# Batch norm and ReLU on one core: the second half of x as one load in the middle, the first half's remainder last

## The chip, the core and the metric

The kernel runs on one core of a Trainium2 chip. The metric is the device time of one execution in microseconds (us). Before the change the median of 8 runs was 83.8 us, from 83.51 to 83.95.

## The reference

`x` is a float32 tensor of shape 32 x 128 x 32 x 32 (16.78 MB). Each of the 128 channels has its own `gamma`, `beta`, `running_mean` and `running_var`:

```python
normalized = (x - running_mean[None, :, None, None]) / np.sqrt(running_var[None, :, None, None] + eps)
scaled = normalized * gamma[None, :, None, None] + beta[None, :, None, None]
return np.maximum(scaled, 0).astype(np.float32)
```

Every element is read once and written once, so 16.78 MB go in and 16.78 MB go out. For each element the work is one multiply, one add and one maximum.

## The kernel before

**Layout.** The tensor is seen as 4096 rows (batch times channel) of `HW` = 1024 floats, 4 KB each. They are split into `T` = 2 halves `t`; in each half, partition `p` of 128 holds `J` = 16 consecutive rows `j`. One partition's 16 rows of a half are 64 KB in one piece of memory. All of `x` fits on the chip at once, so every tile has its own buffer (`bufs=1`), and no load ever waits for a buffer to come free.

**Tiles and loads.** `TILES` lists pieces `(t, a, b)`: rows `a` to `b` of half `t`, in the order in which they are loaded and computed. The sync engine (SP) issues all loads at the start (L56), one DMA per tile, except where `LOAD_CUTS` splits a tile. Before the change there are six loads: of 2, 2, 4 and 8 rows from the first half, and two of 8 rows from the second. In a DMA each partition's rows are one contiguous run, so the six loads consist of runs of 8, 8, 16, 32, 32 and 32 KB, 128 of each.

**Parameters.** The scalar engine (ACT) issues four small DMAs (L63). TensorE spreads the parameters over the partitions (L78), ACT and VectorE (DVE) turn them into a scale and a bias (L86 to L94).

**Compute and stores.** ACT then passes over the rows in the order of `TILES`. One activation, L102, does a row in place (`HALVES` names rows that are done in two halves). After the last row of a tile, or ahead of a row named in `STORE_CUTS`, ACT itself issues the store of the rows since the last store (L110). This order is written out by hand (`manual_schedule`): ACT's queue holds the passes and the store issues in program order. The six stores before the change have runs of 4, 4, 8, 16, 32 and 64 KB per partition; the last is the whole second half.

**Queues.** Loads go through SP's DMA queue (q1 in the profile), stores and parameters through ACT's (q10). Both feed the same 16 DMA engines; each engine serves 8 of the 128 partitions, so a load or a store gives each engine 8 runs. A DMA's completion is counted on one of eight semaphores, used in turn, and a new DMA on a used semaphore waits for that semaphore's previous DMA.

Of the kernel before, what the change touches and what calls it, by code (L numbers as in the profile page):

```python
# [1 line left out]

# [4 lines left out]


F32 = mybir.dt.float32
ACTF = mybir.ActivationFunctionType  # L10

J = 16

TILES = ((0, 0, 2), (0, 2, 4), (0, 4, 8), (0, 8, 16), (1, 0, 16))

LOAD_CUTS = {(1, 8)}
STORE_CUTS = {(0, 1)}

HALVES = {(0, 0), (0, 1)}


@with_exitstack
def kernel(
    ctx: ExitStack,
    tc: tile.TileContext,
    x: bass.AP,
    gamma: bass.AP,
    beta: bass.AP,  # L30
    running_mean: bass.AP,
    running_var: bass.AP,
    eps: bass.AP,
    out: bass.AP,
):
    nc = tc.nc
    B, C, H, W = x.shape
    HW = H * W
    P = nc.NUM_PARTITIONS
    assert C % J == 0 and P % (C // J) == 0 and (B * C) % (P * J) == 0  # L40
    Q = C // J
    T = B * C // (P * J)

    xr = x.rearrange("b c h w -> (b c) (h w)").rearrange("(t p j) w -> t p j w", p=P, j=J)
    outr = out.rearrange("b c h w -> (b c) (h w)").rearrange("(t p j) w -> t p j w", p=P, j=J)

    data = ctx.enter_context(tc.tile_pool(name="data", bufs=1))
    params = ctx.enter_context(tc.tile_pool(name="params", bufs=1))
    psum = ctx.enter_context(tc.tile_pool(name="psum", bufs=1, space=bass.MemoryType.PSUM))

    tiles = []
    for t, a, b in TILES:
        xt = data.tile([P, b - a, HW], F32, name=f"x{t}_{a}")
        cuts = [a] + [j for j in range(a + 1, b) if (t, j) in LOAD_CUTS] + [b]
        for c, d in zip(cuts, cuts[1:]):
            nc.sync.dma_start(out=xt[:, c - a : d - a, :], in_=xr[t, :, c:d, :])  # L56
        tiles.append((t, a, b, xt))

    raw = params.tile([Q, 4, J], F32, name="raw")
    for k, src in enumerate((running_var, gamma, running_mean, beta)):
        nc.scalar.dma_start(out=raw[:, k, :], in_=src.rearrange("(q j) -> q j", j=J))  # L63
    eps_t = params.tile([P, 1], F32, name="eps_t")
    nc.vector.memset(eps_t, float(eps))  # L65
    rep = params.tile([Q, P // Q, Q], F32, name="rep")
    nc.gpsimd.memset(rep, 1.0)  # L67
    nc.gpsimd.affine_select(  # L68
        out=rep,
        in_=rep,  # L70
        compare_op=mybir.AluOpType.is_equal,
        fill=0.0,
        base=0,
        pattern=[[0, P // Q], [-1, Q]],
        channel_multiplier=1,
    )
    cols = psum.tile([P, 4, J], F32, name="cols")
    nc.tensor.matmul(  # L78
        cols.rearrange("p k j -> p (k j)"),
        rep.rearrange("q r s -> q (r s)"),  # L80
        raw.rearrange("q k j -> q (k j)"),
        start=True,
        stop=True,
    )
    std_t = params.tile([P, J], F32, name="std_t")
    nc.scalar.activation(out=std_t, in_=cols[:, 0, :], func=ACTF.Sqrt, bias=eps_t[:, 0:1], scale=1.0)  # L86
    rstd_t = params.tile([P, J], F32, name="rstd_t")
    nc.vector.reciprocal(out=rstd_t, in_=std_t)  # L88
    scale_t = params.tile([P, J], F32, name="scale_t")
    nc.vector.tensor_mul(out=scale_t, in0=cols[:, 1, :], in1=rstd_t)  # L90
    ms_t = params.tile([P, J], F32, name="ms_t")
    nc.vector.tensor_mul(out=ms_t, in0=cols[:, 2, :], in1=scale_t)  # L92
    bias_t = params.tile([P, J], F32, name="bias_t")
    nc.vector.tensor_sub(out=bias_t, in0=cols[:, 3, :], in1=ms_t)  # L94

    with tc.manual_schedule(engines={mybir.EngineType.Activation}):
        for t, a, b, xt in tiles:
            first = a
            for j in range(a, b):
                step = HW // 2 if (t, j) in HALVES else HW  # L100
                for w in range(0, HW, step):
                    nc.scalar.activation(  # L102
                        out=xt[:, j - a, w : w + step],
                        in_=xt[:, j - a, w : w + step],
                        func=ACTF.Relu,
                        bias=bias_t[:, j : j + 1],
                        scale=scale_t[:, j : j + 1],
                    )
                if j + 1 == b or (t, j + 1) in STORE_CUTS:
                    nc.scalar.dma_start(  # L110
                        out=outr[t, :, first : j + 1, :], in_=xt[:, first - a : j + 1 - a, :]
                    )
                    first = j + 1


# [1 line left out]
_INS = ['x', 'gamma', 'beta', 'running_mean', 'running_var', 'eps']  # L117
_OUTS = [((32, 128, 32, 32), 'float32')]

_NUMBERS = {'eps': 1e-05}  # L120


# [26 lines left out]
```

## Time and profile before

| what | value |
|---|---|
| median of 8 runs | 83.8 us (83.51 to 83.95) |
| profiled execution, its own time | 83.45 us |
| span of the profiled execution | 81.7 us |
| ACT busy | 39.1 us (48% of the span) |
| bytes read, written | 16.78 MB, 16.78 MB |
| mean rate over the span | 410 GB/s |
| q1 (loads), share of 16 engines | 48.6% |
| q10 (stores, parameters), share of 16 engines | 47.8% |
| first load issued, last store issued | 0.81 us, 55.98 us |

The span is what the profiler saw of the kernel's instructions; the profiled execution's own time is 1.7 us more. The two shares of the DMA queues add up: each engine serves one queue at a time. All other engines together are busy less than 3 us.

### The profile page before, as it was taken

The page shows a single profiled execution, that of the slowest core. Times are in us where ns is not written, and L with a number is a line of the kernel's source. Part 1 is how long each engine was busy: PE and PEld are TensorE (multiplying, and loading weights), DVE is VectorE, ACT ScalarE, POOL GpSimd, SP SyncE. Part 2 cuts the span into 40 slices and gives each one's busy share as a digit, 9 for nine tenths or more (in the row PEclk, how much of TensorE's full clock was granted, in tenths as well). Part 3 has the DMA queues.
Part 4 walks back from the last instruction along what each step waited for, and adds up shares of the span by engine and source line. Part 5 has one row for each costly group of instructions (what it writes and reads, how often), then busy time and mean ns, then how long its engine had stood idle before and what let it go on. Part 6 is the DMA issues. An engine that isn't in the chain of part 4 may idle for free.

```text
span 81.7 us, 120 instructions
## 1 busy us (share of the span) xinstructions
PE 0.7 (1%) x2; PEld 0.5 (1%) x2; DVE 0.8 (1%) x5; ACT 39.1 (48%) x36; POOL 0.8 (1%) x6
## 2 busy tenths in 40 slices
PE   0003000000000000000000000000000000000000
PEld 0002000000000000000000000000000000000000
DVE  0000300000000000000000000000000000000000
ACT  0600477799239999199995199993000000000000
POOL 3000000000000000000000000000000000000000
DMA  3899999989999999969789699997992999997490
GB/s 44 317 417 481 409 417 481 481 385 463 403 417 449 395 471 393 505 297 601 321 369 593 281 449 425 513 465 305 513 770 96 417 513 513 513 513 321 192 513 0
DMA packets 1792, 33.56 MB, mean 411 GB/s; under 512 B 256, under 2 KB 256, under 8 KB 512
## 3 DMA queue, kind: packets, MB, share of 16 engines
q1 hardware_dynamic: 864, 16.78, 48.6%
q10 hardware_dynamic: 928, 16.78, 47.8%
HBM read 16.78 MB, written 16.78 MB: 410 GB/s over the span
## 4 chain that ended last, share of the span: by engine, by line
DMA 56%; ACT 10%; issue 2%; SPq 0%
DMA x<-in_x_dram 56%; ACT x L102 10%; SPq L56 0%
## 5 line engine op out<-in xcount | busy, mean ns | idle before, releaser
L102 ACT ACTIVATE x<-x,bias_t,scale_t 128x1024 f32<-128x1024 f32 (+1 forms) x34 | 37.5, 1177 | 10.0 <-DMA x<-in_x_dram 7.6
L86 ACT ACT_TABLE_LOAD x1 | 1.3, 1283 | 2.6 <-issue 2.6
L86 ACT ACTIVATE std_t<-cols,eps_t 128x16 f32<-128x16 f32 x1 | 0.3, 274 | 4.3 <-PE cols L78 4.3
L78 PE MATMUL cols<-raw,rep 8*128 8x64 f32 x2 | 0.7, 428 | 7.5 <-DMA raw<-in_beta_dram 7.5
L78 PEld LDWEIGHTS cols<-raw,rep 8*128 8x128 f32 x2 | 0.5, 308 | 7.5 <-issue 7.5
L68 POOL TENSOR_SCALAR_AFFINE_SELECT rep<-rep 8x128 f32<-8x128 f32 x1 | 0.4, 392 | 0.1
L88 DVE RECIPROCAL rstd_t<-std_t 128x16 f32<-128x16 f32 x1 | 0.3, 252 | 7.6 <-ACT std_t L86 7.6
L67 POOL MEMSET rep<- 8x128 f32 x1 | 0.2, 194 | 0.3 <-POOLq L130 0.3
L90 DVE TENSOR_TENSOR scale_t<-cols,rstd_t 128x16 f32<-128x16 f32 x1 | 0.2, 175 | 0.1
L92 DVE TENSOR_TENSOR ms_t<-cols,scale_t 128x16 f32<-128x16 f32 x1 | 0.2, 175 | 0.0
L94 DVE TENSOR_TENSOR bias_t<-cols,ms_t 128x16 f32<-128x16 f32 x1 | 0.2, 175 | 0.0
L130 POOL MEMSET const-bfloat16-1.0<- 128x1 bf16 x1 | 0.1, 107 | 0.0
L130 POOL MEMSET const-uint8-127<- 128x1 uint8 x1 | 0.1, 107 | 0.0
L130 POOL MEMSET const-float32-0.0<- 128x1 f32 x1 | 0.1, 104 | 0.3 <-issue 0.3
L130 POOL MEMSET const-float32-1.0<- 128x1 f32 x1 | 0.1, 104 | 0.0
L65 DVE MEMSET eps_t<- 128x1 f32 x1 | 0.1, 59 | 0.9 <-PEq L130 0.9
## 6 DMA issues: line engine op xcount, KB each, us to landing
x<-in_x_dram SPq DMA_DIRECT2D x3, 4096.0 KB, 38.7
out_dram<-x ACTq DMA_DIRECT2D x1, 4096.0 KB, 28.6
x<-in_x_dram SPq DMA_DIRECT2D x2, 1024.0 KB, 5.8
x<-in_x_dram SPq DMA_DIRECT2D x1, 2048.0 KB, 11.2
out_dram<-x ACTq DMA_DIRECT2D x1, 2048.0 KB
out_dram<-x ACTq DMA_DIRECT2D x2, 512.0 KB, 18.6
out_dram<-x ACTq DMA_DIRECT2D x1, 1024.0 KB
raw<-in_running_var_dram ACTq DMA_DIRECT2D x1, 0.5 KB
```

Source lines behind the costliest of these rows:

```text
L65: nc.vector.memset(eps_t, float(eps))
L67: nc.gpsimd.memset(rep, 1.0)
L68: nc.gpsimd.affine_select(out=rep, in_=rep, compare_op=mybir.AluOpType.is_equal, fill=0.0, base=0, pattern=[[0, P // Q], [-1, Q]], channel ...
L78: nc.tensor.matmul(cols.rearrange("p k j -> p (k j)"), rep.rearrange("q r s -> q (r s)"), raw.rearrange("q k j -> q (k j)"), start=True, s ...
L86: nc.scalar.activation(out=std_t, in_=cols[:, 0, :], func=ACTF.Sqrt, bias=eps_t[:, 0:1], scale=1.0)
L88: nc.vector.reciprocal(out=rstd_t, in_=std_t)
L90: nc.vector.tensor_mul(out=scale_t, in0=cols[:, 1, :], in1=rstd_t)
L92: nc.vector.tensor_mul(out=ms_t, in0=cols[:, 2, :], in1=scale_t)
L94: nc.vector.tensor_sub(out=bias_t, in0=cols[:, 3, :], in1=ms_t)
L102: nc.scalar.activation(out=xt[:, j - a, w : w + step], in_=xt[:, j - a, w : w + step], func=ACTF.Relu, bias=bias_t[:, j : j + 1], scale=sc ...
L130: nc = _bacc.Bacc("TRN2", target_bir_lowering=False, num_devices=1)
```

## The change

`TILES` is put in another order and cut differently. After the two loads of 2 rows, the whole second half (16 rows, runs of 64 KB) is loaded by one DMA. Then rows 4 to 12 of the first half follow (runs of 32 KB), and rows 12 to 16 last (runs of 16 KB). ACT computes and stores in this order; the second half is stored in two DMAs of 8 rows. Row 1 of the first tile is done by one activation instead of two.

```diff
-TILES = ((0, 0, 2), (0, 2, 4), (0, 4, 8), (0, 8, 16), (1, 0, 16))
+TILES = ((0, 0, 2), (0, 2, 4), (1, 0, 16), (0, 4, 12), (0, 12, 16))
 
-LOAD_CUTS = {(1, 8)}
-STORE_CUTS = {(0, 1)}
+LOAD_CUTS = set()
+STORE_CUTS = {(0, 1), (1, 8)}
 
-HALVES = {(0, 0), (0, 1)}
+HALVES = {(0, 0)}
```

There are now five loads, with runs of 8, 8, 64, 32 and 16 KB, and seven stores, with runs of 4, 4, 8, 32, 32, 32 and 16 KB.

## The prediction

> **What bounds the kernel now.** I read the page first: the slices, the queues' shares and the chain.
>
> ```profile
> DMA  3899999989999999969789699997992999997490
> GB/s 44 317 417 481 409 417 481 481 385 463 403 417 449 395 471 393 505 297 601 321 369 593 281 449 425 513 465 305 513 770 96 417 513 513 513 513 321 192 513 0
> ...
> q1 hardware_dynamic: 864, 16.78, 48.6%
> q10 hardware_dynamic: 928, 16.78, 47.8%
> ...
> DMA 56%; ACT 10%; issue 2%; SPq 0%
> ```
>
> The two queues hold the 16 DMA engines for 48.6 + 47.8 = 96.4% of the span, 78.8 us of 81.7. The dips in the slices (6, 2, 4) are no idle time: a run of 64 KB takes longer than a slice of 2.04 us, and 96 GB/s stands right behind 770. The chain is followed through one load and ACT and doesn't show this; its 56% is not the share that DMA bounds. Next the stretches:
>
> ```profile
> 24.00:34.00 10.00, 0.00 (x0) 0.00 (x0) 0.00 (x0) 9.02 (x8) 0.00 (x0) 1.00 0.96 411
> 34.00:46.00 12.00, 0.00 (x0) 0.00 (x0) 0.00 (x0) 9.16 (x8) 0.00 (x0) 1.00 1.01 430
> 46.00:56.00 10.00, 0.00 (x0) 0.00 (x0) 0.00 (x0) 9.16 (x8) 0.00 (x0) 1.00 1.02 437
> 61.00:80.50 19.50, 0.00 (x0) 0.00 (x0) 0.00 (x0) 0.00 (x0) 0.00 (x0) 1.00 0.95 410
> ```
>
> The last two columns are DMA share and GB/s: about 1.0 with loads and stores mixed (24 to 46) and with stores alone. ACT, the fourth busy column, is nearly full up to 56 and then has nothing left, 25 us before the end. The timeline gives the order, and the waits say who waits:
>
> ```profile
> 0.81 7.54 SPq L56 DMA_DIRECT2D x<-in_x_dram  x6
> ...
> 11.05 0.37 ACTq L110 DMA_DIRECT2D out_dram<-x  x1
> ...
> 23.86 9.16 ACT L102 ACTIVATE x<-x,bias_t,scale_t 128x1024 f32<-128x1024 f32 x8 [3.01 <-DMA x<-in_x_dram]
> ...
> 46.80 9.16 ACT L102 ACTIVATE x<-x,bias_t,scale_t 128x1024 f32<-128x1024 f32 x8 [2.84 <-DMA x<-in_x_dram]
> 55.98 0.34 ACTq L110 DMA_DIRECT2D out_dram<-x  x1
> ```
>
> ```profile
> ACT x L102 <- DMA x<-in_x_dram: 7.6, 3, 3.0
> ...
> SPq L144 <- DMA out_dram<-x: 72.4, 4, 38.7
> ```
>
> ACT waits for loads, and the end waits for stores. Everything is issued long before it is moved: all loads by 8.4 us, though the last lands at 46; the last store at 56, though its first run starts at 61. So the bound is the total of the runs on a DMA engine.
>
> The trace's packet records (one for each contiguous run) give that total. A run takes 0.159 us for 4 KB, 0.309 for 8, 0.611 for 16, 1.213 for 32 and 2.418 for 64 KB, as load or store alike (64 KB was only stored). Doubling the size adds twice the bytes at 27.2 GB/s; what is over is some 0.008 us a run. The runs of one engine follow each other without a gap: the first starts at 1.82 us, the last ends at 80.57. That is 78.75 us, made up of 77.90 for its 96 runs at the durations above, 0.55 for the slow first runs before 4 us, 0.20 for 32 KB loads that took longer than 1.213, and 0.10 of gaps. With 1.82 us ahead and 1.18 behind, this is the span of 81.75; with the 1.7 us around it, 83.45, which is 0.35 below the median.
>
> **The change, part by part.** *The runs.* Before, each engine has 8 loads each of 8, 8, 16, 32, 32, 32 KB and 8 stores each of 4, 4, 8, 16, 32, 64: loads 16 x 0.309 + 8 x 0.611 + 24 x 1.213 = 38.94, stores 16 x 0.159 + 8 x (0.309 + 0.611 + 1.213 + 2.418) = 38.95. After, loads are 8 x (0.309 + 0.309 + 2.418 + 1.213 + 0.611) = 38.88, stores 16 x 0.159 + 8 x 0.309 + 24 x 1.213 + 8 x 0.611 = 39.02. Both sums are 77.90: it is the same set of sizes, with the 64 KB runs changed from store to load. Cost zero, if a 64 KB load runs like a 64 KB store.
>
> *64 KB loads.* No row shows one. From above: loads of 32 KB lost 0.20 us over 24 runs of an engine, 0.0083 each, while 8 and 16 KB after the start lost nothing, nor did any store. If the loss grew fourfold with each doubling, the new loads would lose 8 x 0.033 + 8 x 0.0083 = 0.33, 0.13 more than now. The slowest single 32 KB load ran at 23.8 GB/s; all 64 KB loads at that rate (2.76 us) would cost 8 x 0.34 = 2.7 us. From below: the loss goes with reading 32 KB runs, of which 8 remain of 24, which saves 0.13; with the gaps gone too, 0.2. I take zero, since the nearest row, the 64 KB store, runs at full rate (27.1 GB/s), and because the losses came in a few bursts (20.3, 40.0, 44.7 us) in which most engines lost something, not run by run.
>
> *Store issues and ACT.* What could cost is a dry store queue after the last load. Without the store of (1,0:8), an engine has all loads and the three small stores: the first 2 MB end at 7.5 us as now, the other loads take 8 x 4.242 = 33.9, the small stores 16 x 0.159 + 8 x 0.309 = 5.0, so work until 46.4 whatever the order. When does that next store come? The 64 KB loads take 19.3 us, to 26.9; store runs share from some 14.8 (issued at 11.05, the first store's runs began at 14.6 to 14.9), one per load run, five in all, so 27.7. ACT starts 0.7 later (now the last load run ends at 46.09, ACT resumes at 46.80) at 28.4, does 8 passes in 9.16, and issues at 37.6. With a lag of 3.6 (11.05 to 14.6) its first run could start at 41.2: 5.2 us to spare. Its 9.7 us of runs then cover from 46.4 to 56.1; the next store is issued at 47.2, ready at 50.8. The following needs 8 passes more: 56.8, ready 60.4, needed 65.8. The last: 4 passes, 61.8, ready 65.4, needed 75.5. Each has 5 us or more, so nothing on the path. If this cover were gone, each us of lateness would be a us at the end.
>
> How the engines share matters for that margin. In the records, 32 KB load runs alternate with single 4 KB store runs, at times two or three in a row: 16 stores among 17 loads from 13.6 to 35.5 us on one engine. The Trainium skill's page "DMA: Bandwidth & Descriptors", section "Queues, rings and completion order", says instead that an engine takes turns by packets, typically 9 to 17 descriptors. By that rule each small store would leave in one turn, all three during the 64 KB loads. Independently of the rule, the extreme is that all 5.0 us of small stores go ahead of the end of the second half: it ends at 26.9 + 5.0 = 31.9, its store is ready at 45.4 instead of 41.2, and 1.0 us of the margin is left. By row or rule the end stays.
>
> *ACT's passes.* Row 1 in one pass (1.15 us) and not two (1.52 with the gap) advances the second store's issue by 0.3 us; the queue is full of loads then. ACT's long pause up to 28.4 replaces the pauses of 3.0, 1.8 and 2.8. Hidden by the same loads: nothing.
>
> *Issues.* SP issues five loads (0.33 to 0.63 us each). The program's order shows the fourth and fifth waiting for parameter DMAs, which land by 7.5; the queue is filled up to 27 by then. Nothing waits behind them on SP. On ACT, store issues wait for semaphores of the parameters, of loads already computed, and the last for the first store's; all done many us before. The first two loads and the parameters keep their places, so the slow start stays. The last store again uses the semaphore that the last one used, so I leave the 1.18 us of the end alone.
>
> The sum: 0.00 for the runs, 0.00 for the rest, on the profiled 83.45; on the median, 83.8.
>
> **The rivals.**
>
> *Slower: 64 KB loads lose rate.* For: only loads lost anything, and only at the largest size loaded. Against: the 64 KB store has no loss. The place is the 8 runs of an engine between 7.5 and 28 us. From 0.021 us a run (8 x 0.021 = 0.17) it is measurable. At twice the average loss per us of today's 32 KB loads it is the +0.13 above; three times that extra, 0.4, gives 84.2; the far end is 86.5.
>
> *Slower: a dry queue.* For: nothing is stored between 28 and 38. Against: 5 us of margin. It needs ACT or the landing 5 us late; at 6 us late it gives 84.6.
>
> *Faster: the load losses go.* For: they sit in 32 KB loads, of which two thirds go. The full 0.2 and part of the gaps: 83.55. More can't be had, since all else is the runs themselves and the start and end.
>
> *The change isn't what it says:* the program's order shows it as told, so no chance is set aside.
>
> **How the numbers follow.** A measurement can tell about 0.2% (0.17 us) from no change. No change in the end: 0.49. Load losses gone, far enough to be seen: 0.20. 64 KB loads slower: 0.24; dry queue or another late store: 0.07. Faster is thus 0.20, same 0.49, slower 0.31. The forecast's own range is 83.65 to 83.95. For 8 in 10 it reaches down to the full saving and up to the 84.2 of the first rival; left out are its far end and the dry queue.
>
> **What would show it.** Right: runs without gaps from 1.8 to about 80.6, 64 KB loads at 2.42 us, queue shares adding up to 96%, last store issued near 62 with ACT idle behind it, one ACT wait of some 12 us ahead of 28. Wrong: 64 KB loads above 2.44, any engine idle near 46, or a first run later than 1.8.

## The result, and the profile after

The changed kernel takes 84.0 us (median of 22 runs, 83.83 to 84.15); the kernel before, over all its runs here, 83.64 us (62 runs, 83.35 to 84.06). The ratio is 1.004, interval 1.0029 to 1.005: slower by 0.36 us. The profiled execution of the changed kernel took 84.01 us with a span of 82.3.

The page after, with the rows shown of before: the slices, the queues and the chain.

```profile
DMA  2899991999919796969999989997997998998991
GB/s 48 334 427 721 510 446 64 541 541 541 476 66 541 319 542 287 573 287 470 334 414 398 550 350 414 510 478 334 462 494 334 446 510 350 414 510 366 422 406 80
...
q1 hardware_dynamic: 720, 16.78, 48.8%
q10 hardware_dynamic: 1072, 16.78, 47.5%
...
ACT 36%; DMA 32%; issue 3%; ACTq 1%; SPq 1%
```

The queues' shares still add up to 96.3%; the low slices early on (64 and 66 GB/s) follow high ones and are the 64 KB loads, booked by their start. The chain now walks through ACT, which is not the bound. The timeline and the two waits:

```profile
28.43 9.16 ACT L102 ACTIVATE x<-x,bias_t,scale_t 128x1024 f32<-128x1024 f32 x8 [13.04 <-DMA x<-in_x_dram]
37.61 0.34 ACTq L110 DMA_DIRECT2D out_dram<-x  x1
...
47.19 0.34 ACTq L110 DMA_DIRECT2D out_dram<-x  x1
...
56.76 0.34 ACTq L110 DMA_DIRECT2D out_dram<-x  x1
...
61.81 0.34 ACTq L110 DMA_DIRECT2D out_dram<-x  x1
```

```profile
ACT x L102 <- DMA x<-in_x_dram: 13.0, 1, 13.0
...
SPq L144 <- DMA out_dram<-x: 73.7, 4, 49.7
```

The end of ACT's pause and the four store issues are where the prediction's working put them, to 0.1 us. The difference is in the stretches (same columns as before: DMA share and GB/s last):

```profile
24.00:34.00 10.00, 0.00 (x0) 0.00 (x0) 0.00 (x0) 5.58 (x5) 0.00 (x0) 1.00 0.96 406
34.00:46.00 12.00, 0.00 (x0) 0.00 (x0) 0.00 (x0) 11.58 (x12) 0.00 (x0) 1.00 0.98 397
46.00:56.00 10.00, 0.00 (x0) 0.00 (x0) 0.00 (x0) 9.58 (x10) 0.00 (x0) 1.00 1.05 454
```

From 34 to 46 us the engines are as occupied as before (0.98), but move 397 GB/s where they moved 430. (Runs are booked where they start, so a few per cent of this are the edges of the stretch.) The packet records give the exact sum. *Nominal* is each run at its duration from the trace of before; *load loss* below is always what the loads after 4 us took beyond 0.309, 0.611, 1.213 and 2.418 us a run. "Per engine" is a sixteenth of the sum over all records. Two profiles of each kernel, the second ones from the experiments:

| us per engine | before | before again | after | after again |
|---|---|---|---|---|
| first run to last end | 78.75 | 78.92 | 79.33 | 79.24 |
| nominal sum of the 96 runs | 77.90 | 77.90 | 77.90 | 77.90 |
| slow runs before 4 us | 0.55 | 0.48 | 0.47 | 0.46 |
| load loss after 4 us | 0.20 | 0.43 | 0.77 | 0.70 |
| gaps, engines not ending together | 0.10 | 0.11 | 0.19 | 0.18 |

On average the time from first run to last end, below called the *transfer time*, grew by 0.45 us, of which 0.42 is load loss. What lies outside it did not change: the profiled execution's own time less the transfer time is 4.70 and 4.69 us before, 4.68 and 4.69 after. Stores lost nothing in any of the four. In the changed kernel the loss sits at few places: 0.16 and 0.19 at the eighth 64 KB run (25 us), and 0.57 and 0.44 in the 16 KB runs between 38.8 and 46.3 us. The 32 KB loads between lost 0.00 and 0.03.

### The profile page after: what moved, and what is told of

Read it like the earlier page. It is cut to its first block, busy times and chain, and to the rows that moved or that the text cites. A ratio compares the mean times of both kernels' runs of the same rounds, so it can differ in the third digit from the quotient of the medians.

```text
span 82.3 us, 119 instructions
## 1 busy us (share of the span) xinstructions
PE 0.7 (1%) x2; PEld 0.6 (1%) x2; DVE 0.8 (1%) x5; ACT 38.8 (47%) x35; POOL 0.8 (1%) x6
## 4 chain that ended last, share of the span: by engine, by line
ACT 36%; DMA 32%; issue 3%; ACTq 1%; SPq 1%
ACT x L102 36%; DMA x<-in_x_dram 32%; ACTq L110 1%; SPq L56 1%
```

## The experiments

The first theory to test was S (64 KB load runs lose rate), against M (short load runs lose where they meet short store runs) and T (stalls at moments of their own).

The variants differ in one more thing. By their profiles, the time outside the transfer time is 4.7 us in both kernels, e2 and e4, but 4.9 in e1, e3, e8, e12, f2, f3 and f4, 4.95 in e9, 5.0 in e7, 5.1 in e10 and f1 and 5.2 in e11. Up to 0.5 us of a variant's time, more than the effect of the change, is thus not in its runs; why is not known. What bears on the cause is the load loss, not the ratio.

**e1: the 64 KB load as two of 32 KB.**

```diff
-LOAD_CUTS = set()
+LOAD_CUTS = {(1, 8)}
```

> The changed kernel with the second half loaded by two DMAs with runs of 32 KB instead of one with 64 KB; all else as changed. Theory S (64 KB load runs lose rate): the loss between 7 and 28 us (0.19 us an engine in the changed kernel's packet records) goes to near 0, and the time falls by about 0.2 us, to 83.8. Theory M (16 KB load runs lose where they take turns with short store runs at the end of the loads, 0.57 us an engine): no change there, time stays at 84.0 (0.4% above before). Theory T (stalls of all engines at moments of their own, whatever the runs): same loss in total, 84.0.

Measured 84.28 us, ratio 1.0092 (1.0064 to 1.012): slower still; 0.2 us of the further 0.28 lies outside the transfer time. The load loss is 0.83, all of it in 32 KB runs, 0.00 in the 16 KB ones, though some of these ran between 8 KB stores. S failed, and M with it.

**e2: rising sizes at the end.**

```diff
-TILES = ((0, 0, 2), (0, 2, 4), (1, 0, 16), (0, 4, 12), (0, 12, 16))
+TILES = ((0, 0, 2), (0, 2, 4), (1, 0, 16), (0, 4, 8), (0, 8, 16))
```

> The changed kernel with the first half's remainder loaded as 4 rows and then 8 (runs of 16 KB, then 32 KB) instead of 8 and then 4. Theory M: the last load runs, which meet the 8 KB stores, are now 32 KB ones, the 16 KB ones meet 4 KB stores at 28 to 33 us; the 0.57 us falls to 0.2 or less and the time to 83.6 to 83.7. Theory S: 64 KB loads are still there, 84.0. Theory T: 84.0.

Measured 83.88 us, 1.0033 (1.002 to 1.0046). The loss, 0.63, moved on: 0.19 at the eighth 64 KB run again, 0.36 at the eighth and last 32 KB run. The falling sizes cost at most some 0.1 us.

**e3: the kernel before, second half as one 64 KB load.**

```diff
-LOAD_CUTS = {(1, 8)}
+LOAD_CUTS = set()
```

> The kernel before with the second half loaded by one DMA (64 KB runs) at the end; order and stores as before. Theory S: 8 runs of 64 KB lose some 0.2 us an engine beside the 0.1 that 32 KB loads lose now, time 0.1 to 0.2 us above before. Theory M: the loads keep long runs to the end, same as before within 0.1 us. Theory T: as before.

Measured 87.01 us, 1.0409 (1.0386 to 1.0432); no theory had it. Its timeline, and a stretch of it:

```profile
45.43 18.21 ACT L102 ACTIVATE x<-x,bias_t,scale_t 128x1024 f32<-128x1024 f32 x16 [12.47 <-DMA x<-in_x_dram]
63.66 0.34 ACTq L110 DMA_DIRECT2D out_dram<-x  x1
```

```profile
62.00:64.50 2.50, 0.00 (x0) 0.00 (x0) 0.00 (x0) 1.63 (x2) 0.00 (x0) 1.00 0.00 0
```

With nothing of the second half landed before 45 us, ACT needs 18.2 us until its one store, and the engines stand still from 62.2 to 64.5. This is the dry queue: some 2.4 us of the 3.4. Most of the rest is load loss, 1.05, of which 0.89 at the last 64 KB run; 0.2 lies outside the transfer time.

**e4: the small stores held back** to the first store of the second half (`HELD` names them).

```diff
+HELD = {(0, 1), (0, 2), (0, 4)}
...
+                    if (t, j + 1) not in HELD:
+                        for dst, src in held:
+                            nc.scalar.dma_start(out=dst, in_=src)
```

> The changed kernel with its three small stores (rows 0, 1 and 2 to 4) held back and issued with the first store of the second half, at some 37 us, so that loads run alone up to 39 us or so and hardly any load run meets a store run. Theories M and T in the form that loads lose only beside stores: the loss of loads after 4 us falls from 0.77 us to under 0.2 and the time to 83.4 to 83.5, below before. Theory S: the loss of the 64 KB runs, 0.19, stays, since it is due to their size; 83.6. If stalls come at moments of their own and hit loads alone as well: 84.0.

Measured 84.06 us, 1.0052 (1.0033 to 1.0072). The hold worked otherwise than meant:

```profile
27.84 1.24 ACT L105 ACTIVATE x<-x,bias_t,scale_t 128x1024 f32<-128x1024 f32 x1 [13.34 <-DMA x<-in_x_dram]
27.92 1.35 ACTq L117 DMA_DIRECT2D out_dram<-x  x3
```

The three stores stand behind eight passes in program order, but were issued when the first of these had just begun: they wait only for their own rows. Still it shows something: while loads ran alone, to 31.7 us, the 64 KB and 32 KB runs lost 0.00. From there to the end of the loads 0.36 were lost. The median stayed near the changed kernel's because first runs (0.64) and unequal ends (0.50 with the gaps) took what the loads saved.

**e5, e6: both kernels profiled again.**

> The changed kernel itself, profiled a second time. Theory T (stalls come at moments of their own): the long load runs stand elsewhere than at 24.9, 40.1 and 44.1 us, and their sum differs from 0.77 us an engine by some tenths. Theory P (stalls follow from which runs are read and written together): the same runs are long again (the eighth 64 KB load, the third and sixth or so of the 16 KB loads), with about the same sum.

> The kernel before itself, profiled a second time. Theory P: the loss of its loads after 4 us is again near 0.20 us an engine, in small pieces near 20, 40 and 44.5 us. Theory T: the pieces stand elsewhere and the sum is anything between 0.1 and 0.6 us (its times spread over 0.7 us, from 83.35 to 84.06).

The runs are the same, their losses vary (table above): after, 25 and 40 us again (0.19, and 0.30 for 0.25), 44 us with 0.05 for 0.22; before, 0.05 at 20 us both times, 0.22 for 0.03 at 40. The times were 83.93 and 83.61. T in the form of moments unrelated to the runs falls; the place follows the sequence, the amount only partly. Fixed moments counted from the start would repeat too; against them stand f2 and e10 below, in which loads and stores ran side by side to 51.9 and 54.5 us and lost 0.00 after 30 us.

**e7: small stores behind the first store of the second half**, which does wait for its passes (e4 with the held stores in another order).

```diff
+                        for dst, src in held[-1:] + held[:-1]:
```

> The changed kernel with its three small stores issued behind the first store of the second half, which itself waits for eight passes: nothing is stored before some 39 us, and loads run alone until then. If loads lose only beside stores: no loss from 8 to 39 us, in all at most 0.2 us an engine, and the time is 83.4 to 83.6, at or a little below before. If loads lose by themselves (by size, or at moments of their own): some 0.5 us or more is lost and the time stays at 84.0.

Measured 85.12 us, 1.0165 (1.014 to 1.0191). Loads alone from 8 to 37 us lost 0.00, as the first reading said; then 1.3 us were lost at once, not the 0.2 at most of that reading. Two stretches:

```profile
28.00:36.00 8.00, 0.00 (x0) 0.00 (x0) 0.00 (x0) 8.00 (x8) 0.00 (x0) 1.00 0.97 418
...
38.00:42.00 4.00, 0.00 (x0) 0.00 (x0) 0.00 (x0) 3.36 (x3) 0.00 (x0) 1.00 1.06 315
```

Engines fully occupied at 315 GB/s: that is a load loss seen on a view. Stores were issued from 36.7 us, but the first store run started at 41.1. The 16 KB load runs five to seven, the last ones ahead of an engine's first 32 KB store run, took about 1.0 us on average in place of 0.61. Of the 1.35 us, 0.84 were lost in load runs that had ended before any store run began: store runs beside them can't be what made these long.

**e8: the order alone**, with the load sizes of before.

```diff
-TILES = ((0, 0, 2), (0, 2, 4), (1, 0, 16), (0, 4, 12), (0, 12, 16))
+TILES = ((0, 0, 2), (0, 2, 4), (1, 0, 16), (0, 4, 8), (0, 8, 16))
-LOAD_CUTS = set()
+LOAD_CUTS = {(1, 8)}
```

> The order alone: the second half ahead of the first half's last 12 rows, but with the load sizes of the kernel before (32 KB twice for the second half, then 16 KB and 32 KB). If the place of the second half carries the loss: 0.5 us or more an engine in loads and 84.0 or above. If the sizes carry it (64 KB in the middle, 16 KB at the end): 0.2 us and 83.6 as before.

Measured 84.31 us, 1.0076 (1.0053 to 1.0099), load loss 0.71. With after, e1 and e2 this makes a square:

| ratio to before | last loads 32, 16 KB | last loads 16, 32 KB |
|---|---|---|
| second half as one 64 KB load | 1.004 (the change) | 1.0033 (e2) |
| second half as two 32 KB loads | 1.0092 (e1) | 1.0076 (e8) |

In load loss the same four are 0.77 and 0.70 (the change), 0.63 (e2), 0.83 (e1) and 0.71 (e8), against 0.20 and 0.43 before: the order carries the loss. The single 64 KB load takes back only some 0.1 us of it, less than the two profiles of before differ (0.23). The upper row is faster by 0.3 to 0.4 us in good part for another reason: by the profiles, e1 and e8 spend 0.2 us more outside the transfer time. Falling or rising makes no clear difference.

**e9: no overlap.** The kernel before, all stores held behind one of the second half's first six rows, in e7's order of issue.

```diff
+HELD = {(0, 1), (0, 2), (0, 4), (0, 8), (0, 16)}
-STORE_CUTS = {(0, 1)}
+STORE_CUTS = {(0, 1), (1, 6)}
```

> The kernel before (its loads and their order) with all stores held until six rows of the second half are done, at some 39.4 us; a store of those six rows goes first, the five others behind it, the remaining ten rows last. Loads run alone to their end at some 41. If all loss of loads comes from stores beside them: under 0.1 us an engine lost in loads, at most some 0.5 us of dry engines between loads and stores, and the time within 0.2 us of before, 83.4 to 83.8. If the start of a store lets loads lose by itself (over 1 us was lost in the late variant around the issue of four stores): the loss comes again at 40 us, up to 1.3 us, and the time is 84.3 to 85.

Measured 83.76 us, 1.0013 (0.9992 to 1.0035): no different from before. The first store run started at 41.2 us, just as the loads ended; load loss 0.045, no gap there. So the loss comes with stores that are issued while loads run: in all 18 profiles the loads lost at most 0.06 us before the first store was issued, in the 8 KB runs of the start. Without the loss the kernel was still no faster, since the engines started and ended further apart (0.31 with the gaps, for 0.11) and 4.95 us lay outside the transfer time, for 4.7.

**e10, e11: the three small stores as one of 16 KB runs**, in both kernels. The edit for the changed kernel; before likewise:

```diff
-TILES = ((0, 0, 2), (0, 2, 4), (1, 0, 16), (0, 4, 12), (0, 12, 16))
+TILES = ((0, 0, 4), (1, 0, 16), (0, 4, 12), (0, 12, 16))
-LOAD_CUTS = set()
+LOAD_CUTS = {(0, 2)}
-STORE_CUTS = {(0, 1), (1, 8)}
+STORE_CUTS = {(1, 8)}
```

> The changed kernel with its three small stores as one store of rows 0 to 4 (8 runs of 16 KB an engine in place of 24 runs of 4, 4 and 8 KB). Theory F (loads lose where a new store DMA is brought in behind the running one): one boundary in place of three beside the loads, loss of 0.3 us or less instead of 0.70 to 0.77, time 83.6. Theory P without that (only which bytes are read and written together): no forecast of sign, a loss between 0.2 and 0.8 at other places, 83.5 to 84.1.

> The kernel before with its three small stores as one store of rows 0 to 4. Theory F: loss falls from 0.20 to 0.43 us to 0.15 or less, time 83.4, below before by 0.1 to 0.3 us. Theory P without that: anything between 83.4 and 84.

Changed kernel: 84.5 us, 1.0097 (1.0071 to 1.0122), load loss 0.90: 0.28 in the run ahead of the first store run, 0.58 at the eighth 64 KB run. Kernel before: 90.37 us, 1.0796 (1.0766 to 1.0827). There the larger store runs take longer turns, the last load lands late, and the one 8 MB store comes at 66.6 us behind a dry queue:

```profile
57.43 9.16 ACT L102 ACTIVATE x<-x,bias_t,scale_t 128x1024 f32<-128x1024 f32 x8 [7.80 <-DMA x<-in_x_dram]
66.61 0.34 ACTq L110 DMA_DIRECT2D out_dram<-x  x1
```

```profile
62.00:67.50 5.50, 0.00 (x0) 0.00 (x0) 0.00 (x0) 4.58 (x5) 0.00 (x0) 1.00 0.20 83
```

That is 5.4 us without any run, and 1.06 of load loss. F, fewer stores brought in means less loss, falls. Of the changed kernel's extra 0.5 us here, 0.4 lies outside the transfer time.

**e12: the sizes of e8 in sequence, other rows.**

```diff
-TILES = ((0, 0, 2), (0, 2, 4), (1, 0, 16), (0, 4, 12), (0, 12, 16))
+TILES = ((0, 0, 2), (0, 2, 4), (0, 4, 12), (1, 0, 8), (0, 12, 16), (1, 8, 16))
```

> The sizes of loads and stores in the sequence of the order-alone variant (loads of 8, 8, 32, 32, 16, 32 KB; stores of 4, 4, 8, 32, 32, 16, 32 KB), but with other rows: rows 4 to 12 of the first half, 8 rows of the second, rows 12 to 16 of the first, 8 rows of the second. If the sequence of sizes and times carries the loss of the order-alone variant: loads lose 0.6 to 0.8 us again, at the same runs (seventh and eighth of the third load, 14 to 17 us; sixth and seventh of the 16 KB load), 84.3. If it is that the second half is read first while the first half is written: loss 0.2 to 0.45, 83.6 to 83.8.

Measured 84.3 us, 1.0086 (1.0054 to 1.0119), load loss 0.74 against 0.71, at the same runs (mean excess of a run, us):

| load run | e8 | e12 |
|---|---|---|
| third load (32 KB), seventh and eighth | 0.20, 0.06 | 0.14, 0.03 |
| fourth load (32 KB), eighth | 0.11 | 0.09 |
| fifth load (16 KB), sixth and seventh | 0.12, 0.15 | 0.05, 0.19 |
| sixth load (32 KB), seventh | 0.06 | 0.21 |

The runs are the same and so is the sum; the amounts at a run differ by up to three times. Which half is read while which is written thus plays no part that shows here. The sequence of sizes in the two queues does: that is what "the order" in the square stands for.

**f1 to f4: what of the stores counts.**

```diff
 f1, after:   STORE_CUTS = {(0, 1), (0, 3), (1, 8)}
 f2, after:   STORE_CUTS = {(1, 8)}
 f3, before:  STORE_CUTS = {(0, 1), (0, 3)}
 f4, e7:      only the newest store is issued at each point, the held ones behind row 16 of the second half
```

> The changed kernel with rows 2 and 3 stored by one DMA each: the small stores are four DMAs with 4 KB runs. Theory R (a load run loses by the size of the store run that comes in behind it): the 0.25 us ahead of the 8 KB store goes, loss of loads 0.3 to 0.5 us an engine, time 83.7 to 83.8. Theory F (it loses by the number of store DMAs brought in beside loads): four instead of three, loss 0.75 us or more, 84.0 to 84.2.

> The changed kernel with rows 0 and 1 stored by one DMA: the small stores are two DMAs with 8 KB runs. Theory R: between the changed kernel (0.70 to 0.77 us, 84.0) and the one store with 16 KB runs (0.90, 84.5): loss 0.8 to 0.9, 84.1 to 84.4, some of it now ahead of the first store at 14 us. Theory F: two instead of three, loss 0.5 us, 83.8.

> The kernel before with rows 2 and 3 stored by one DMA each. Theory R: the loss at the 8 KB runs (0.09 to 0.25 us around 40 us) goes, 0.1 to 0.15 us are left, time 83.4 to 83.6, at or below before. Theory F: one store DMA more, loss 0.3 to 0.5, 83.7 to 83.9.

> The late variant, with the first store of 8 rows of the second half alone at some 36.7 us; the three small stores follow the next store at 47 us. Theory R (32 KB store runs behind 16 KB loads): 1.0 to 1.3 us are lost at 38 to 42 us as with four issues, time 84.8 to 85.1. If four issues in a row did it: 0.3 us or less, 83.9 to 84.1.

| kernel | us | ratio (interval) | load loss |
|---|---|---|---|
| f1: 4, 4, 4, 4 KB | 84.61 | 1.011 (1.0087 to 1.0133) | 0.92 |
| the change: 4, 4, 8 KB | 84.0 | 1.004 (1.0029 to 1.005) | 0.77, 0.70 |
| f2: 8, 8 KB | 84.11 | 1.006 (1.0036 to 1.0084) | 0.65 |
| e10: 16 KB | 84.5 | 1.0097 (1.0071 to 1.0122) | 0.90 |
| f3: before with 4, 4, 4, 4 KB | 84.4 | 1.009 (1.0069 to 1.0111) | 0.83 |
| f4: one late store | 84.93 | 1.015 (1.0123 to 1.0177) | 1.23 |

In f4, one store of 32 KB runs costs what four issues in a row did, at the same 16 KB load runs: the issues aren't it. But f1 and f3 refute R as stated: ahead of the 4 KB store that replaced the 8 KB one there is indeed no loss, yet 0.71 appear later, at the sixth and seventh 16 KB load run (f1), and 0.43 at the last 32 KB run (f3). Neither the number of store DMAs nor the size of their runs orders these losses alone. The same bytes in the same order, with one DMA cut in two, move and resize them.

**What stays open.** Shown: loads lose, stores hardly do (0.00 in both kernels, at most 0.08, in e3 and e11); loads lose nothing to speak of until a store is issued, then beside store runs or, as in e7 and f4, in the runs just ahead of the first one; it happens at particular runs, mostly the sixth to eighth of a load DMA or the runs just ahead of the first run of a newly arrived store; it repeats with the sequence of sizes and not with the rows. The most regular is the eighth and last run of a 64 KB load: in all seven profiles where it ran beside stores it lost (0.13 to 0.89 us). An issued store is needed but not enough: 16 KB loads between 8 KB stores lost 0.3 us in the changed kernel, 0.00 in e1 and f2. Not settled is which part of the chip makes those runs long. Nearly all 16 engines lose at the same runs, so the records can't tell a cause inside each engine from one that they share. Nor, since the records of an engine follow each other without a gap, whether the time belongs to the load or to the change to what comes behind it. A relation between the partition being loaded and the one being stored wasn't separated either: e12 kept it.

## Why the prediction was wrong

**Held.** The runs: nominal sums equal, 77.90 and 77.90. Start and end: first run at 1.79 (1.82 before), 1.18 us behind the last end in both. Store issues at 37.61, 47.19, 56.76 and 61.81, for 37.6, 47.2, 56.8 and 61.8. The store queue was never dry: the first run of the 37.61 store started at 46.7. ACT's pause of 13.0 us was hidden. Engines alternated single runs as the trace of before showed, 64 KB loads with 4 KB stores one for one. The Trainium skill's page "DMA: Bandwidth & Descriptors" (section "Queues, rings and completion order") has turns of several descriptors instead; they were seen no more than before, and the trace decides.

**The step that failed** is the load losses, under "64 KB loads". The working let 0.20 us stand as it was and took zero for the change; measured were 0.77 and 0.70 where before had 0.20 and 0.43, and that difference is the result. Two reasons given there were wrong. "Because the losses came in a few bursts ... not run by run" read them as moments unrelated to the runs; e5, e6 and e12 show that they belong to particular runs in a sequence. And the working looked only at the one size that was new. More than half of the loss came in the 16 KB loads, of which it said that this size "lost nothing": in the trace of before they had all ended before the first store run. The 0.20 was also a single draw; the same kernel gave 0.43 the next time, so the base was uncertain by more than half of the effect that was denied. The base of the forecast was off as well: 83.8 was the median of 8 runs, 83.64 that of 62, so a change that cost nothing would have come out at 83.64.

**The rivals.** "64 KB loads lose rate" was priced up to 84.2, near what came, but for a wrong reason: alone, these runs lost 0.00 (e4, e7, f4), in the changed kernel beside stores 0.19 and 0.22, no more than the 32 KB loads of before (0.20 and 0.41), and splitting them did not lower the loss (e1). "A dry queue" did not happen in the changed kernel and did in e3 and e11, where the store of the second half was one piece and came late; before had the same one piece, in time. In the changed kernel one piece could have been issued at 47.2 us at the earliest, with 46.4 us of other work by the prediction's sum; that its two-part store keeps it safe follows from this, but was not run. That all of the load losses might go, the faster rival, is what e9 tried: 0.045 were left, and 83.76 us were no gain, since other terms grew.

## What to carry to other kernels

When the transfer engines are occupied from end to end, a rearranged sequence of the same bytes can change what is lost inside the runs and what passes outside them, so add up, run by run, what the trace's transfers took beyond their clean duration, in more than one profile, before calling such a change free. Take the time outside the transfers apart from it: between variants here it differed by up to 0.5 us. Loads that ran clean alone say nothing about loads beside stores: cost the overlap from stretches where both run, and give it an uncertainty of its own. And before making transfers larger, ask when the last of them can be computed and stored: in e3 and e11 this cost 2.4 and 5.4 us, far more than anything that run sizes did.

## What the runs showed of the hardware that was not expected

Once stores are issued, a load run can take some 60 to 75% longer than alone (16 KB: about 1.0 us on average against 0.61 in e7), with the engine shown as busy all the while, and even before the first store run begins.

A store that stands behind passes in ACT's program order is not held by them: in e4 it was issued 0.08 us after the first of eight passes began.

Issuing stores can become slow; why is not shown. In e9 the six held stores took 8.3 us to issue (0.4 us for the first, 2.9 for the second, 1.2 for each other; 0.34 when alone), and ACT's next pass waited for it; the four of e7 took 1.9 us:

```profile
39.42 8.33 ACTq L117 DMA_DIRECT2D out_dram<-x  x6
47.80 11.42 ACT L105 ACTIVATE x<-x,bias_t,scale_t 128x1024 f32<-128x1024 f32 x10 [8.41 <-issue]
```
